# The query projection of a hybrid attention block in three product tiles per four heads, with the scaled latent split

## The chip, the cores and the metric

The kernel runs on one core of one Trainium2 chip. The time is device time in microseconds (us) of one execution, lower is better. TensorE (PE) makes the matrix products, VectorE (DVE), ScalarE (ACT) and GpSimd (POOL) the elementwise work, SyncE (SP) issues the DMAs. "PEld" in a profile is TensorE's weight load, which overlaps the products.

## The reference, cut to what matters

Two layers, each: half-step FFN, mixer, half-step FFN. The mixer of a layer reads one input `h` and makes latent attention (8 heads) beside a recurrent branch; 128 context tokens and 256 latent tokens are kept side by side as 384 columns. The part that is changed:

```
c_q, c_kv, k_rope, u_x, u_g = split(h @ w_in)
q = rms_norm(c_q, q_norm_g) @ w_uq              # 384 -> 8 heads x (64 + 32)
q_nope, q_rope = q[..., :64], q[..., 64:]
# latent tokens only:
apply_rope(x): x1, x2 = x[:16], x[16:]
               concat(x1*cos - x2*sin, x1*sin + x2*cos)
s = q_nope . k_nope + q_rope . k_rope           # then softmax, @ v
```

`rms_norm` divides by the root mean square of a token's 384 latent values and multiplies by `g`.

## The kernel before, in words

Activations are stored transposed: features on the 128 partitions, 384 tokens along the free axis (`T`). Every fp32 product is made of three rounded ones: `piece` (L307) splits a weight tile into a high part `wh` (cast on ScalarE, L315) and a low part `wl` (subtraction on VectorE, L316), activations are split in the same way, and `mm3` (L319 to L322) makes high x high, high x low and low x high. Weights come through `stage` buffers (`ws`, three of them) by DMAs that SP issues (L295); the splits go to `split_pool` (three each).

The order of the work on each engine is not written by hand: a scheduler orders the instructions by program order as a priority and its own plan of the times, and assigns buffers; each engine then works through its own list in order. Splits are marked as urgent (`PIECE_AHEAD`). A "pump" makes the modulation vectors (`gm` products from `wm`, L238) in steps that the scheduler puts between other products.

Products go to PSUM tiles: four `acc` tiles (tag `acc`), three `ms` tiles, one `gm` tile. Temporary tiles of 384 columns share the tag `t1` (three buffers): the gate branch's `gu`, the rotary product `qr`, the latent's `cq`.

The mixer in program order: the convolution and the recurrent branch (`lru`, advanced by `next(lru)` between other parts); the key/value latent; the rotary key (`krm`, `kr`); the query latent; the gate branches 0 and 1; `keys(0)`, `queries(0)`, `values()`, the gate branches 2 and 3; then the attention over head pairs, with `keys(1)` and `queries(1)` in front of the third pair; the pump's steps; the output projection (`w_o`).

The query latent, before: three chunks, each multiplied by `g` (L660) and split at once (`cqh` L661, `cql` L662), while the squares go to `token_scale`, which sums them over the partitions, takes the power on GpSimd (L352) and spreads the factor `pr` over the partitions by a product (L555). The factor is not put on the latent but on the projected queries: `rr` is the rotary table `tab` times `pr` (L665).

`queries(hf)`, before: each of four heads has a tile of 128 rows: 64 plain rows, 32 rotary ones, and the same 32 with their halves swapped, which GpSimd copies into the weights (`turn_q`, L700, L701). So a head is one product tile of three chunks, nine products, and on VectorE:

```
nc.vector.tensor_tensor(t2[64:96, P:T], ps[96:128, P:T], rr[96:128, P:T], op=ALU.mult)
nc.vector.tensor_tensor(q[0:96, :], ps[0:96, :T], rr[0:96], op=ALU.mult)
nc.vector.tensor_tensor(q[64:96, P:T], q[64:96, P:T], t2[64:96, P:T], op=ALU.add)
```

The scores (L772) then take 96 rows of `qT` and `kT`; the maxima are L773, the exponentials L778. The 32 rotary rows of `kT` are copied from `kr` by DMAs on SP (L713).

## Time and profile before

| what | value |
|---|---|
| time, median of 3 runs | 1603.82 us (1603.72 to 1605.43) |
| the profiled execution | 1606.49 us, its span 1604.7 us |
| TensorE busy | 1551.7 us, 97% of the span |
| VectorE / ScalarE / GpSimd busy | 946.9 / 659.4 / 161.3 us |
| mean granted clock of TensorE | 0.984 |

Times inside the profile are microseconds from the start of its span. Products overlap each other, so the shown duration of one is longer than the distance to the next.

### The profile page before, as it was taken

The numbers are of one execution on the slowest core, as the hardware profiler recorded it, in microseconds if no ns is written. First come the engines' busy times: TensorE is split into PE (matmuls) and PEld (weight loads), VectorE is DVE, ScalarE is ACT, GpSimd is POOL, SyncE is SP. The second block draws the span as 40 slices with busy tenths as digits, with TensorE's granted clock in tenths as the row PEclk, the third lists the DMA queues.
The fourth block names the chain that finished last, engine by engine and source line by source line (L and its number), as shares of the span: only waits on it lengthen the run. The fifth ranks groups of instructions, "written<-read, shape, count | busy, mean of one in ns | idle before, by whom it ended". The sixth has DMA issues, their size and how long they took to land.

```text
span 1604.7 us, 22948 instructions
## 1 busy us (share of the span) xinstructions
PE 1551.7 (97%) x9234; PEld 1453.5 (91%) x9234; DVE 946.9 (59%) x1568; ACT 659.4 (41%) x1068; POOL 161.3 (10%) x142
## 2 busy tenths in 40 slices
PE   6999999999999999999999999999999989999997
PEld 5999999988668999999989999998866789999996
DVE  3778754477986947864364444346788664344334
ACT  4533333268743633333243333234775444333321
POOL 0000002220004100001120000033000140000011
PEclk9999999999999999999989999999999989999998
DMA  9865553447644445553444333335654223433331
GB/s 308 268 231 188 181 200 125 117 143 244 208 156 158 159 158 181 200 191 126 141 157 156 108 132 125 125 105 171 201 186 146 74 65 125 144 120 129 120 118 40
DMA packets 214790, 249.93 MB, mean 156 GB/s; under 512 B 26394, under 2 KB 193308, under 8 KB 211612
## 3 DMA queue, kind: packets, MB, share of 16 engines
q1 hardware_dynamic: 214684, 248.47, 46.5%
q8 instruction: 72, 1.18, 0.3%
q14 instruction: 34, 0.28, 0.1%
HBM read 245.52 MB, written 1.88 MB: 154 GB/s over the span
## 4 chain that ended last, share of the span: by engine, by line
PE 91%; DVE 4%; DMA 2%; ACT 1%; POOL 1%; issue 1%; SPq 0%; DVEq 0%; ACTq 0%; POOLq 0%
PE acc L320 27%; PE acc L322 27%; PE acc L321 27%; PE gm L238 3%; PE acc L772 1%; PE ms L392 1%; DVE wl L316 1%; PE pv L805 1%; DMA wm<-in_w_mod_dram 1%; DMA ws<-in_w_ffn_up_dram 1%; PE ms L788 1%; PE ms L320 1%; PE ms L321 0%; PE ms L322 0%; POOL sum_f L378 0%
## 5 line engine op out<-in xcount | busy, mean ns | idle before, releaser
L315 ACT CAST wh<-ws 128x1024 fp32r<-128x1024 f32 (+1 forms) x332 | 336.3, 1014 | 755.3 <-PE acc L321 523.0
L316 DVE TENSOR_TENSOR wl<-ws,wh 128x1024 fp32r<-128x1024 f32 (+1 forms) x332 | 411.5, 1240 | 376.9 <-ACT wh L315 373.7
L320 PE MATMUL acc<-hh,wh 128*128 128x384 f32 x1280 | 428.8, 338 | 10.5 <-ACT hh L278 7.4
L322 PE MATMUL acc<-hh,wl 128*128 128x384 f32 x1280 | 431.9, 338 | 2.4 <-DVE wl L316 2.4
L321 PE MATMUL acc<-hl,wh 128*128 128x384 f32 x1280 | 432.5, 338 | 0.4 <-DVE hl L286 0.4
L320 PEld LDWEIGHTS acc<-hh,wh 128*128 128x128 f32 x1280 | 241.6, 189 | 17.7 <-ACT hh L278 8.6
L322 PEld LDWEIGHTS acc<-hh,wl 128*128 128x128 f32 x1280 | 243.3, 190 | 6.4 <-DVE wl L316 2.9
L321 PEld LDWEIGHTS acc<-hl,wh 128*128 128x128 f32 x1280 | 243.2, 190 | 2.6 <-issue 1.3
L320 PE MATMUL acc<-gh,wh 128*128 128x384 f32 x704 | 236.7, 336 | 0.0
L321 PE MATMUL acc<-gl,wh 128*128 128x384 f32 x704 | 236.3, 336 | 0.0
L322 PE MATMUL acc<-gh,wl 128*128 128x384 f32 x704 | 236.0, 335 | 0.0
L320 PEld LDWEIGHTS acc<-gh,wh 128*128 128x128 f32 x704 | 132.1, 188 | 0.4 <-issue 0.4
L321 PEld LDWEIGHTS acc<-gl,wh 128*128 128x128 f32 x704 | 132.3, 188 | 0.0
L322 PEld LDWEIGHTS acc<-gh,wl 128*128 128x128 f32 x704 | 132.1, 188 | 0.0
L492 DVE TENSOR_TENSOR a<-a,acc 128x384 f32<-128x384 f32 x87 | 48.2, 554 | 122.6 <-PE acc L322 117.7
L252 DVE SCALAR_TENSOR_TENSOR gsum<-wm,sil,gsum 128x512 f32<-128x512 f32 x168 | 120.0, 766 | 0.0
L320 PE MATMUL acc<-hh_in,wh 128*128 128x384 f32 x336 | 112.0, 339 | 5.2 <-ACT hh_in L278 5.0
L321 PE MATMUL acc<-hl_in,wh 128*128 128x384 f32 x336 | 113.0, 336 | 0.0
L322 PE MATMUL acc<-hh_in,wl 128*128 128x384 f32 x336 | 112.7, 336 | 0.0
L377 POOL TENSOR_TENSOR sum_f<-X 128x384 f32<-128x384 f32 x4 | 5.1, 1281 | 829.5 <-DVE X L368 829.5
L320 PEld LDWEIGHTS acc<-hh_in,wh 128*128 128x128 f32 x336 | 63.0, 189 | 7.1 <-ACT hh_in L278 6.1
L238 PE MATMUL gm<-wm,sil 128*32 128x128 f32 (+2 forms) x640 | 62.1, 446 | 4.3 <-DMA wm<-in_w_mod_dram 2.0
(268 smaller groups left out, 1750.2 us busy)
## 6 DMA issues: line engine op xcount, KB each, us to landing
ws<-in_w_ffn_up_dram SPq DMA_DIRECT2D x84, 1024.0 KB, 5.1
wm<-in_w_mod_dram SPq DMA_DIRECT2D x56, 1024.0 KB, 5.4
ws<-in_w_ffn_down_dram SPq DMA_DIRECT2D x32, 1024.0 KB, 5.2
wm<-in_w_mod_dram SPq DMA_DIRECT2D x32, 512.0 KB, 5.1
ws<-in_w_ffn_down_dram SPq DMA_DIRECT2D x16, 768.0 KB, 4.5
ws<-in_w_in_dram SPq DMA_DIRECT2D x12, 1024.0 KB, 6.1
ws<-in_w_o_dram SPq DMA_DIRECT2D x8, 1024.0 KB, 5.3
ws<-in_w_ffn_up_dram SPq DMA_DIRECT2D x8, 384.0 KB, 6.7
```

Of the source, the lines that this page charges most:

```text
L238: nc.tensor.matmul(self.ps[32 * g : 32 * g + 32, :n], lhsT, wv[:, g], start=self.fresh, stop=stop)
L252: nc.vector.scalar_tensor_tensor(self.sum[:, r], wv[:, kk], s, self.sum[:, r], op0=ALU.mult, op1=ALU.add)
L315: nc.scalar.copy(parts[0], src)
L316: nc.vector.tensor_tensor(parts[1], src, parts[0].bitcast(F32), op=ALU.subtract)
L320: nc.tensor.matmul(ps, wh, xh, start=start, stop=False)
L321: nc.tensor.matmul(ps, wh, xl, start=False, stop=False)
L322: nc.tensor.matmul(ps, wl, xh, start=False, stop=stop)
L392: nc.tensor.matmul(self.pt[:, 2 * i + j : 2 * i + j + 1], src[:, i * P : (i + 1) * P], mean_w[:, 0:1], start=False, stop=stop and i == T / ...
L492: nc.vector.tensor_tensor(a, a, px[:, :T], op=ALU.mult)
L772: nc.tensor.matmul(views[i], qT[hf][0:96, h % 4, q0 : q0 + P], kT[hf][0:96, h % 4, k0:k1], start=True, stop=True)
L788: nc.tensor.transpose(t0[:, (2 * j + i) * P : (2 * j + i + 1) * P], pr_[:, (0, 512)[i] + j * P : (0, 512)[i] + (j + 1) * P], ident)
L805: nc.tensor.matmul(o[:, P:T], v, pTs[e][:, (j - 1) * 256 : j * 256], start=(j == 1), stop=(j == 3))
```

## The change

The query latent is kept in fp32 (`cq32`, three `t1` tiles) until `pr` is there, is multiplied by it, and only then split; `rr` is gone. The weights of four heads come in one DMA of whole rows. Of four heads the 64 plain rows are taken two heads per product tile (two tiles), and the rotary rows of all four heads in a third tile, first halves in rows 0 to 63, second halves in rows 64 to 127. Plain rows are copied to `qT` (VectorE and ScalarE one each per tile); the rotary tile is turned with `cos` and `sin` tables over all 128 partitions, and eight DMAs that GpSimd issues put 16 rows each at their places in `qT`. `cos` and `sin` are built from `tab` by twelve DMAs on GpSimd's queue in place of one load on SP's. The rotary key uses the new tables, with the sign of one half put on its weight.

```diff
+    def split(parts, n):
+        n_w[0] += 1
+        th, tl = (split_pool.tile([P, 1024], F32R, tag=tag, name=f"{tag}{n_w[0]}") for tag in ("wh", "wl"))
+        with tc.high_priority(offset=PIECE_AHEAD):
+            for src, view in parts:
+                nc.scalar.copy(view(th[:, :n]), src)
+                nc.vector.tensor_tensor(view(tl[:, :n]), src, view(th[:, :n]).bitcast(F32), op=ALU.subtract)
+        return th[:, :n], tl[:, :n]
...
             def turn(ws):
                 v = ws[:, : KD * P].rearrange("p (k c) -> p k c", c=P)
                 nc.gpsimd.tensor_copy(v[:, :, 96:112], v[:, :, 80:96])
-                nc.gpsimd.tensor_copy(v[:, :, 112:128], v[:, :, 64:80])
+                nc.gpsimd.tensor_scalar(v[:, :, 112:128], v[:, :, 64:80], -1.0, None, op0=ALU.mult)
...
                 nc.vector.tensor_scalar_mul(h32, ps[:, :T], g)
+                cq32.append(h32)
+                next(lru)
+            pr = token_scale(sqs, sel_q, RMS_EPS, f"q{l}")
+            for j, h32 in enumerate(cq32):
+                nc.vector.tensor_tensor(h32, h32, pr[:, :T], op=ALU.mult)
                 nc.scalar.copy(cqh[:, j, :], h32)
                 nc.vector.tensor_tensor(cql[:, j, :], h32, cqh[:, j, :].bitcast(F32), op=ALU.subtract)
-                next(lru)
-            pr = token_scale(sqs, sel_q, RMS_EPS, f"q{l}")
-            nc.vector.tensor_tensor(rr, tab, pr[:, :T], op=ALU.mult)
...
             def queries(hf):
...
+                q = qT[hf]
+                n = 4 * (DN + DR)
+                w = load_w([(lambda t: t[:, : 3 * n].rearrange("p (k c) -> p k c", c=n), w_uq[:, :, n * hf : n * hf + n])])
+                w = w[:, : 3 * n].rearrange("p (k h e) -> p k h e", k=3, h=4)
+                wh, wl = split([(w[:, :, :, :DN], lambda t: t.rearrange("p (k h e) -> p k h e", k=3, h=4))], 3 * 4 * DN)
...
+                for j in range(2):
                     ps = acc_tile()
                     for k in range(3):
-                        mm3(ps[:, :T], wh[:, k, o : o + P], wl[:, k, o : o + P], cqh[:, k, :], cql[:, k, :], k == 0, k == 2)
...
+                        mm3(ps[:, :T], wh[:, k, j * P : (j + 1) * P], wl[:, k, j * P : (j + 1) * P], cqh[:, k, :], cql[:, k, :], k == 0, k == 2)
+                    nc.vector.tensor_copy(q[0:64, 2 * j, :], ps[0:64, :T])
+                    nc.scalar.copy(q[0:64, 2 * j + 1, :], ps[64:128, :T])
+                wh, wl = split([(w[:, :, :, DN + 16 * x : DN + 16 * x + 16],
+                                 lambda t, x=x: t.rearrange("p (k x h e) -> p k x h e", k=3, x=2, h=4)[:, :, x]) for x in range(2)], 3 * P)
...
+                t1, t2 = (tmp.tile([P, T], F32, tag="t1", bufs=3, name=f"qr{i}{l}{hf}") for i in range(2))
+                nc.vector.tensor_tensor(t1, ps[:, :T], cos, op=ALU.mult)
+                nc.vector.tensor_tensor(t2[0:64, P:T], ps[64:128, P:T], sin[64:128, P:T], op=ALU.mult)
+                nc.vector.tensor_tensor(t2[64:128, P:T], ps[0:64, P:T], sin[0:64, P:T], op=ALU.mult)
+                nc.vector.tensor_tensor(t1[:, P:T], t1[:, P:T], t2[:, P:T], op=ALU.add)
+                for h in range(4):
+                    for x in range(2):
+                        nc.gpsimd.dma_start(q[64 + 16 * x : 80 + 16 * x, h, :], t1[64 * x + 16 * h : 64 * x + 16 * h + 16])
...
-    tab = const.tile([P, T], F32, name="tab")
-    nc.sync.dma_start(tab, A["tab"])
+    cos, sin = (const.tile([P, T], F32, name=n) for n in ("cos", "sin"))
+    for i in range(4):
+        nc.gpsimd.dma_start(cos[32 * i : 32 * i + 32], A["tab"][64:96])
+    for i in range(8):
+        r0 = 112 if i < 4 else 96
+        nc.gpsimd.dma_start(sin[16 * i : 16 * i + 16], A["tab"][r0 : r0 + 16])
```

## Rows read from the trace of the kernel before

**Rows 1.** The page: engines' busy time, and the chain that ended last.
```profile
PE 1551.7 (97%) x9234; PEld 1453.5 (91%) x9234; DVE 946.9 (59%) x1568; ACT 659.4 (41%) x1068; POOL 161.3 (10%) x142
...
PE 91%; DVE 4%; DMA 2%; ACT 1%; POOL 1%; issue 1%; SPq 0%; DVEq 0%; ACTq 0%; POOLq 0%
```

**Rows 2.** TensorE's timeline, layer 0, second query group: start, duration, instruction.
```profile
452.11 0.44 PE L320 MATMUL acc<-cqh,wh 128*128 128x384 f32 x1
...
458.51 1.25 PE L772 MATMUL acc<-kT,qT 96*128 96x128 f32 x6
```

**Rows 3.** Windows: busy time per engine (instructions), granted clock, DMA share, GB/s.
```profile
400.00:420.00 20.00, 19.18 (x104) 14.89 (x103) 18.63 (x32) 17.77 (x26) 1.26 (x2) 1.00 0.60 210
460.00:475.00 15.00, 14.72 (x83) 7.61 (x76) 12.83 (x38) 7.94 (x28) 0.00 (x0) 1.00 0.70 253
1246.00:1260.00 14.00, 11.01 (x50) 6.70 (x49) 11.54 (x35) 6.09 (x24) 0.00 (x0) 0.88 0.17 60
```

**Rows 4.** TensorE's waits in layer 1's mixer: total, times, longest.
```profile
PE acc L772 <- ACT p L778: 1.9, 1, 1.9
...
PE acc L772 <- DVE qT L739: 1.0, 1, 1.0
```

**Rows 5.** TensorE's timeline, layer 0, first query group; in brackets idle time and releaser.
```profile
410.09 0.45 PE L320 MATMUL acc<-cqh,wh 128*128 128x384 f32 x1 [0.59 <-DVE gu L679]
...
418.19 0.47 PE L320 MATMUL acc<-wh,ckh 128*128 128x512 f32 x1 [0.23 <-DVE qT L739]
...
429.36 1.90 PE L772 MATMUL acc<-kT,qT 96*128 96x128 f32 x8
```

**Rows 6.** VectorE's groups by form: count, busy time, mean ns, idle time before.
```profile
L316 DVE TENSOR_TENSOR wl<-ws,wh 128x768 fp32r<-128x768 f32 x48 | 45.9, 957 | 110.2 <-ACT wh L315 110.2
...
L739 DVE TENSOR_TENSOR qT<-acc,rr 96x384 f32<-96x384 f32 x16 | 8.9, 554 | 0.2
...
L738 DVE TENSOR_TENSOR qr<-acc,rr 32x256 f32<-32x256 f32 x16 | 6.8, 428 | 1.6 <-PE acc L322 1.0
L740 DVE TENSOR_TENSOR qT<-qT,qr 32x256 f32<-32x256 f32 x16 | 6.7, 420 | 0.4
...
L710 DVE COPY kT<-acc 64x512 f32<-64x512 f32 x8 | 5.4, 679 | 2.3 <-PE acc L322 2.3
...
L662 DVE TENSOR_TENSOR cql<-cq,cqh 128x384 fp32r<-128x384 f32 x6 | 3.3, 548 | 0.1
```

**Rows 7.** VectorE's timeline, layer 0, around the query latent's factor.
```profile
396.52 0.55 DVE L679 SCALAR_TENSOR_TENSOR gu<-gu,acc 128x384 f32<-128x384 f32 x1
398.34 0.56 DVE L665 TENSOR_TENSOR rr<-tab,ms 128x384 f32<-128x384 f32 x1 [1.27 <-PE ms L555]
...
401.01 0.96 DVE L316 TENSOR_TENSOR wl<-ws,wh 128x768 fp32r<-128x768 f32 x1 [0.32 <-ACT wh L315]
...
403.23 0.68 DVE L710 COPY kT<-acc 64x512 f32<-64x512 f32 x1 [0.80 <-PE acc L322]
```

**Rows 8.** One line of the kernel, SP's copies of `kr`: duration of issue, time to landing.
```profile
L713 SPq DMA_DIRECT2D kT<-kr x16: 571/588/624, 366.6 to 1230.9; - x16
...
DMA to landing us min/median/max: 2.0/3.0/5.8
```

**Rows 9.** Timelines of ScalarE (layer 0, layer 1) and VectorE (layer 1), second group's softmax.
```profile
463.94 0.37 ACT L778 ACTIVATE p<-acc,mx 128x128 f32<-128x128 f32 x1 [4.36 <-DVE mx L774]
...
1250.29 0.37 ACT L778 ACTIVATE p<-acc,mx 128x128 f32<-128x128 f32 x1 [4.28 <-DVE mx L774]
...
1247.73 2.32 DVE L773 TENSOR_REDUCE mx<-acc 128x1 f32<-128x384 f32 x5
```

**Rows 10.** TensorE's timeline, layer 0, among the second group's scores.
```profile
462.99 1.92 PE L238 MATMUL gm<-wm,sil 128*32 128x512 f32 x14
```

**Rows 11.** The opening: a window as in rows 3, and the chain in time order.
```profile
0.00:40.00 40.00, 27.21 (x321) 23.61 (x321) 13.89 (x48) 16.73 (x31) 0.68 (x6) 1.00 0.93 308
...
17.00 8.88 DMA ws<-in_w_ffn_up_dram
```

More of the change, by code (lines that the diff above doesn't have):

```diff
@@ L565, in mixer @@
             kr = mp.tile([P, 512], F32, name=f"kr{l}")
-            rr = mp.tile([P, T], F32, name=f"rr{l}")
             ckh = mp.tile([P, 2, 512], F32R, name=f"ckh{l}")
@@ L646, in mixer @@
             next(lru)
-            sqs = []
+            sqs, cq32 = [], []
             for j in range(3):
@@ L695, in mixer @@
             w_kv = load_w(parts).rearrange("p (k s c) -> p k s c", k=2, s=2)
-            w_uq = A["w_uq"][l].rearrange("(k p) (h e) -> p k h e", p=P, h=H)
-            def turn_q(ws):
-                v = ws[:, :1536].rearrange("p (x e) -> p x e", e=P)
-                nc.gpsimd.tensor_copy(v[:, :, 96:112], v[:, :, 80:96])
-                nc.gpsimd.tensor_copy(v[:, :, 112:128], v[:, :, 64:80])
+            w_uq = A["w_uq"][l].rearrange("(k p) c -> p k c", p=P)
             def keys(hf):
@@ L725, in queries @@
                 qT[hf] = qkv.tile([P, 4, T], F32, tag="qT", name=f"qT{l}{hf}")
-                parts = [(lambda t, k=k: t[:, k * 512 : (k + 1) * 512].rearrange("p (h e) -> p h e", e=P)[:, :, :96],
-                          w_uq[:, k, 4 * hf : 4 * hf + 4]) for k in range(3)]
-                w = load_w(parts, turn_q)[:, :1536].rearrange("p (k c) -> p k c", k=3)
-                for j in range(4):
-                    if j % 2 == 0:
-                        wh, wl = piece(w[:, :, j * P : (j + 2) * P])
-                    o = (j % 2) * P
+                q = qT[hf]
@@ L733, in queries @@
+                n = 4 * (DN + DR)
+                w = load_w([(lambda t: t[:, : 3 * n].rearrange("p (k c) -> p k c", c=n), w_uq[:, :, n * hf : n * hf + n])])
+                w = w[:, : 3 * n].rearrange("p (k h e) -> p k h e", k=3, h=4)
+                wh, wl = split([(w[:, :, :, :DN], lambda t: t.rearrange("p (k h e) -> p k h e", k=3, h=4))], 3 * 4 * DN)
+                wh, wl = (x.rearrange("p (k c) -> p k c", k=3) for x in (wh, wl))
+                for j in range(2):
                     ps = acc_tile()
@@ new lines, in queries @@
+                    nc.vector.tensor_copy(q[0:64, 2 * j, :], ps[0:64, :T])
+                    nc.scalar.copy(q[0:64, 2 * j + 1, :], ps[64:128, :T])
+                wh, wl = split([(w[:, :, :, DN + 16 * x : DN + 16 * x + 16],
+                                 lambda t, x=x: t.rearrange("p (k x h e) -> p k x h e", k=3, x=2, h=4)[:, :, x]) for x in range(2)], 3 * P)
+                wh, wl = (x.rearrange("p (k c) -> p k c", k=3) for x in (wh, wl))
+                ps = acc_tile()
+                for k in range(3):
+                    mm3(ps[:, :T], wh[:, k], wl[:, k], cqh[:, k, :], cql[:, k, :], k == 0, k == 2)
```

9 lines of the change are left out of this document (2 added, 7 removed).

## The prediction

> **What bounds the kernel now.** I read the page first. TensorE is busy 97% of the span and the chain that ended last runs on it for 91% [rows 1]: what leaves the chain must be TensorE work, and what returns must be a wait of TensorE. The two mixers hold the whole change, so I then read TensorE in order of time through the first one. A product of 384 columns shows about 0.34 us, but such instructions overlap. The pace is what counts: 36 of them run from 452.11 to the first scores at 458.51 [rows 2], so 6.40 / 36 = 0.178 us each. The reader should see that a removed product is worth 0.178 us, not 0.34.
>
> Third, the waits. In the 15 us of that second group's scores TensorE idles 0.28 us in layer 0 (15.00 - 14.72); in layer 1 it idles 2.99 of 14 us and the mean granted clock is 0.88 [rows 3]. There the waits are for the softmax's exponentials on ScalarE (1.9 us) and for `qT` (1.0 us) [rows 4]: a chain of latencies, not TensorE's work, sets that stretch. Fourth, the stretch of the first query group: VectorE is busy 18.63 of 20 us and TensorE 19.18 [rows 3]. Two engines are near full there, and the only waits of TensorE from 404 us to the first scores are for VectorE to give back a PSUM tile: 0.59 us for the gate branch's `gu`, 0.23 us for `qT` [rows 5].
>
> **The change, part by part.** *TensorE.* Per four heads the before kernel makes four product tiles (nine products each), the changed one three. Over two groups and two layers that is 4 x 9 = 36 products less: 36 x 0.178 = **-6.4 us**. This is certain as work, and as time only while TensorE doesn't wait instead.
>
> *VectorE behind the products.* Before, each tile costs 0.428 + 0.554 + 0.420 us [rows 6], 5.6 us per four heads. After: two plain copies (at most the 0.68 us of the `kT` copy [rows 6], which has more columns; I take 0.55), one multiplication over 384 columns (0.55), two over 256 (0.43 each), one sum (0.42): 2.9 us. The other two plain copies go to ScalarE, which is less full than VectorE there [rows 3]. The weight split shrinks from 2 x 768 columns (0.957 each [rows 6]) to 768 and 2 x 192; a 192-column split isn't in the trace, it lies between 0 and the 0.957 of 768 columns; by its length I take 0.3. So VectorE gains some 3 us per four heads. That is worth only the 0.23 us wait for `qT` in the first group [rows 5]: **-0.2 us**. The weights come in one transfer instead of three and lose two GpSimd copies; both finish long before use, so nothing is gained.
>
> *The latent, scaled and then split.* The factor reaches VectorE at 398.34 [rows 7]. Before, the three splits of `cq` were long done and only one multiplication followed (`rr`, 0.56). After, three multiplications (0.554 each, as `qT`'s of 384 columns [rows 6]), three ScalarE casts and three subtractions (0.548 [rows 6]) come behind it: 3 x 0.554 + 3 x 0.548 - 0.56 = 2.75 us more VectorE in exactly the full stretch. It also keeps all three `t1` buffers until then, so the first gate branch's two steps (2 x 0.55 us, the last at 396.52 [rows 7]) slide behind it too: 3.85 us. VectorE has idle spots of 0.32 and 0.80 us there [rows 7], which leaves 2.7 us. Queued behind are the `kT` copies, the scans and the second `gu`; for that one a query tile waits until 410.09 (0.59 us [rows 5]), and for want of a PSUM tile TensorE can only do pump products meanwhile. Bounds per layer: 0 (the wait is filled) and 3.85 us; I take half of 2.7, since the order is planned anew and ScalarE's `kT` copies free two other tiles: 2 x 1.35 = **+2.7 us**.
>
> *Rotary rows by DMA.* New: behind the rotary product 0.55 + 2 x 0.43 + 0.42 = 1.83 us of VectorE, then eight GpSimd DMAs of 16 partitions, two per head. The trace has no DMA issued by GpSimd; the nearest row is `kT` from `kr` on SP: 0.59 us per issue, 3.0 us to landing, 5.8 at most [rows 8]. First group: the products end about 415, the first scores start at 429.36 [rows 5]. 1.8 + 8 x 0.59 + 3.0 = 9.5 us fit into 14: hidden by the value and gate products; without that cover it would be the second group's case. There nothing lies between. Layer 1: the products end at 1244.94 - 1.6 = 1243.3, VectorE at 1245.2, the first head's two transfers at 1245.2 + 0.6 + 3.0 = 1248.8, then scores and maxima, some 2.5 us (by 1247.73, where five maxima begin, and the exponentials at 1250.29 [rows 9]), so exponentials at 1251.3 against 1250.29. That is 1.0 later instead of 1.6 earlier: +2.6. Layer 0: 458.51 - 1.6 + 1.8 + 3.6 = 462.3, exponentials at 464.8 against 463.94 [rows 9]; but the pump's products stand among the scores there (14 of 512 columns at 462.99 [rows 10]) and TensorE hardly idles, so they fill the wait: 0. Together **+2.6 us**, between 0 and the late case below. Behind the DMAs on GpSimd's queue come only the residual's sums, after the attention; each copy of `t1` is held until its DMAs have landed, and nothing but two gate branches asks for one of the other two.
>
> The Trainium skill (DMA: Bandwidth & Descriptors, Anatomy of one DMA — SWDGE (gpsimd) path) gives a GpSimd DMA a fixed 2.0 us plus a bytes term, by which 24 KB land in an estimated 2.1 us; the row of an SP transfer says 3.0, no row here shows GpSimd's, and by the page the sum would be 0.9 us less.
>
> *Opening.* `tab` (one SP load behind the opening's weights) becomes twelve GpSimd loads, 256 rows of 1536 bytes, 393 KB together. GpSimd has nothing else then, so they may start with the first weights, where the DMA engines move 308 GB/s at a share of 0.93 and the chain waits 8.88 us for an up-projection load [rows 11]. 393 KB / 308 GB/s = 1.28 us; bounds 0 and 1.28, I take half: **+0.6 us**. The key's sign flip costs GpSimd one instruction in place of another of the same size: 0.
>
> **Sum.** -6.4 - 0.2 + 2.7 + 2.6 + 0.6 = -0.7 us. The profiled execution took 1606.49 us (span 1604.7), 2.67 above the median; -0.7 on it is 1605.8, and on the median 1603.82 it is **1603.1 us**.
>
> **Rivals.**
> *The saving comes through.* The planner finds products for both first-group waits, and layer 1's transfers cost only 1.0 us: -6.4 - 0.2 + 1.0 + 0.6 = -5.0, **1598.8 us**. For it: TensorE is the bound almost everywhere [rows 1], and VectorE gets lighter. Against: the waits have hardly any work but the pump that needs no PSUM tile.
> *Late rotary rows (slower).* If GpSimd issues at 1.2 us and lands at the slowest row's 5.8 [rows 8], the second group's first head is ready 1.2 + 5.8 behind VectorE: 7.0 instead of 3.6: exponentials at 1254.7 and 468.2, 4.4 and 4.3 later than now, so +6.0 and, with the pump used up, +5.9: -6.4 - 0.2 + 2.7 + 11.9 + 0.6 = +8.6, **1612.4 us**. It decides from about 4.3 us of issue and landing in both layers (the sum passes +3.2 there). For it: both layers have the scores directly behind, and layer 1's stretch already shows a granted clock of 0.88, so a longer wait may cost clock too. Against: `kT`'s median is half of it.
> The Trainium skill (SBUF — State Buffer, SBUF: two separate sides) speaks for this case: VectorE operations in a two-port mode lock GpSimd out, so that it can't write descriptors, and a transfer of 620 ns took 3100. No row here shows a GpSimd DMA beside VectorE.
> *VectorE's queue in full.* Both first groups wait the whole 3.85, and the opening the whole 1.28: -6.4 - 0.2 + 7.7 + 2.6 + 1.3 = +5.0, **1608.8 us**. For it: VectorE at 18.63 of 20 us [rows 3].
> *No effect of the change at all* is excluded: 36 products are gone from the list.
>
> **Chances.** Forecast (part given back) 0.42, saving comes through 0.31, VectorE's queue 0.12, late rows 0.15. A measurement of this kernel can tell 0.2%, 3.2 us. Faster: 0.31 and 0.03 of the forecast's spread, 0.34. Slower: 0.15 and 0.08 of the queue's case, 0.23. Within: the rest, 0.43. The range has to reach into both signs: 1597.0 (a little under the second case, since its +1.0 may be 0) to 1609.5 leaves out about 0.08 below and 0.12 above. The forecast's own range is 1600 to 1606.
>
> **What would show it.** Right: 108 instead of 144 products from `cqh` and `cql`; a wait of 1 to 3 us before the second query tile in both layers, its releaser VectorE; the first scores of layer 1's second group some 5 us behind the last query product, waiting for a DMA; the first group's scores not waiting. Wrong: GpSimd issues or landings far from 0.6 and 3.0 us; another releaser than a `gu` step near 410; scores of layer 0's second group idling TensorE; the twelve table loads not in the opening; or a new order that moves waits into stretches the change doesn't touch.

## The result, and the profile after

The changed kernel takes 1632.03 us (median of 4, 1625.30 to 1633.14) beside 1604.39 us for the kernel before on the same chip: ratio 1.0153, interval 1.0138 to 1.0168. It is slower: by some 25 us by the ratio and between the two profiled executions (spans 1629.7 and 1604.7 us), by 27.6 between the medians. Forecast were 1603.1 us, a range from 1597.0 to 1609.5, and a chance of 0.23 for slower. The range did not hold the time.

The page of the changed kernel, engines' busy time and the chain that ended last:

```profile
span 1629.7 us, 22947 instructions
...
PE 1554.8 (95%) x9198; PEld 1453.9 (89%) x9198; DVE 935.0 (57%) x1552; ACT 661.6 (41%) x1080; POOL 179.7 (11%) x178
...
PE 91%; DVE 3%; ACT 2%; DMA 2%; POOL 1%; issue 1%; SPq 0%; DVEq 0%; POOLq 0%; ACTq 0%
```

Beside [rows 1]: TensorE runs 36 products fewer and is busy 3 us longer, in a span 25 us longer. Less work has become more busy time, so the products themselves got slower (an estimate: 36 products fewer at 0.175 us should have taken 6.3 us off, so some 9.4 us are new); and some 22 us are new idle time (span less busy: 74.9 against 53.0). To see where, I took the first product of each stage from the timelines of both kernels:

| stretch, us | before | changed | before, with rotary rows by transfer (12) | changed, rotary tile first (9) | as 9, products for transfers and loads (14) |
|---|---|---|---|---|---|
| opening, to the first down-projection product | 221.7 | 225.9 | 223.2 | 225.4 | 222.1 |
| to the first query product | 182.7 | 182.3 | 183.5 | 183.8 | 184.6 |
| layer 0, first query to last output product | 111.3 | 126.6 | 121.8 | 111.3 | 108.0 |
| to layer 1's first query product | 673.7 | 673.2 | 670.3 | 669.7 | 670.4 |
| layer 1, first query to last output product | 111.6 | 118.8 | 121.9 | 114.8 | 110.3 |
| the rest of the span | 303.7 | 302.9 | 304.3 | 303.0 | 303.8 |

(The last three columns are experiments below.) Of the 25 us, 15.3 are lost in layer 0's mixer, 7.2 in layer 1's, 4.2 in the opening; the rest gives 1.7 back. TensorE's waits in the changed kernel (total, times, longest):

```profile
PE acc L789 <- DMA qT<-qr: 15.5, 2, 9.0
...
PE acc L330 <- ACT kT L717: 5.3, 2, 2.6
```

These two lines are new: the scores waiting for the rotary rows' transfers, once per layer, and a product waiting for ScalarE's copy of `kT`, once per layer. The two mixers as windows (columns as in [rows 3]), of the kernel before:

```profile
404.40:515.70 111.30, 109.05 (x607) 84.52 (x606) 92.95 (x186) 54.72 (x116) 19.97 (x14) 0.98 0.52 178
1189.40:1301.00 111.60, 105.91 (x590) 83.29 (x588) 83.09 (x171) 54.97 (x116) 18.39 (x14) 0.98 0.36 121
```

and of the changed kernel:

```profile
408.20:534.80 126.60, 113.33 (x609) 85.76 (x608) 90.02 (x186) 59.05 (x124) 25.54 (x28) 0.93 0.53 176
1208.00:1326.80 118.80, 107.07 (x578) 83.21 (x576) 79.46 (x166) 59.16 (x124) 25.54 (x28) 0.94 0.35 117
```

Window less busy PE (its first figure) is idle time; one less the granted clock, times the window, is about what the half level took (an estimate: at 1.2 GHz a product of the first group goes at 0.32 us instead of 0.175, shown below). Layer 0: idle 13.27 against 2.25, +11.0; clock 0.07 x 126.6 - 0.02 x 111.3, +6.6. Layer 1: idle 11.73 against 5.69, +6.0; clock 7.1 - 2.2, +4.9. But these two terms overlap. Part of the half level falls on the long waits themselves, where TensorE has no work to slow down; two windows inside the waits:

```profile
472.40:478.20 5.80, 0.00 (x1) 0.04 (x1) 2.39 (x5) 0.00 (x0) 2.97 (x7) 0.50 1.06 354
1267.70:1272.00 4.30, 0.00 (x0) 0.00 (x0) 1.34 (x2) 0.00 (x0) 2.31 (x5) 0.50 0.73 239
```

Half of their lengths, 2.9 and 2.2 us, is counted twice and comes off the clock, which leaves +3.7 and +2.7 (an estimate). Eighteen query products less are worth -3.2 in each layer. That makes +11.5 of the 15.3 measured in layer 0 and +5.5 of 7.2 in layer 1. Most of the rest is work that the new order moved into these stretches: 14 more pump products in layer 0 (86 instead of 72) and six more products of the recurrent branch in each layer (an estimate: 22 pump products take 2.77 us in layer 0 of the kernel before, a product of the branch 0.175, so 2.8 and 1.0 us). So the saving is there, and waits and the clock take it back several times over; about a quarter of that loss in layer 0 and a third in layer 1 is clock, the rest is waiting.

Cut at the first scores of each mixer, the part ahead of them (the first group, from the first query product on) grew by 5.7 us in layer 0 and 4.9 in layer 1, the part behind them by 9.6 and 2.3. Layer 0's first group as a window, before and changed:

```profile
404.40:429.30 24.90, 24.08 (x134) 20.02 (x133) 24.45 (x47) 18.08 (x30) 1.26 (x2) 1.00 0.63 214
408.20:438.90 30.70, 28.07 (x147) 21.62 (x146) 24.15 (x47) 21.48 (x35) 3.96 (x8) 0.94 0.81 266
```

**Layer 0's second group.** TensorE's timeline of the changed kernel, which answers to [rows 2]:

```profile
467.04 0.33 PE L332 MATMUL acc<-cqh,wl 128*128 128x384 f32 x1
467.31 1.92 PE L238 MATMUL gm<-wm,sil 128*32 128x512 f32 x16
478.20 2.04 PE L789 MATMUL acc<-kT,qT 96*128 96x128 f32 x4 [8.97 <-DMA qT<-qr]
```

The last query product, sixteen pump products, and then nothing for 8.97 us. VectorE's timeline of that gap:

```profile
467.90 0.55 DVE L751 TENSOR_TENSOR qr<-acc,cos 128x384 f32<-128x384 f32 x1
468.46 0.43 DVE L752 TENSOR_TENSOR qr<-acc,sin 64x256 f32<-64x256 f32 x1
468.90 0.42 DVE L753 TENSOR_TENSOR qr<-acc,sin 64x256 f32<-64x256 f32 x1
469.35 1.23 DVE L316 TENSOR_TENSOR wl<-ws,wh 128x1024 fp32r<-128x1024 f32 x1
470.49 0.42 DVE L754 TENSOR_TENSOR qr<-qr,qr 128x256 f32<-128x256 f32 x1
```

The four operations cost what was forecast (1.82 against 1.83 us), but a weight split of 1024 columns stands between the third and the fourth. Then GpSimd's timeline, where one line is the eight transfers' issue together:

```profile
471.56 3.81 POOL L757 DMA_DIRECT2D qT<-qr  x8 [41.27 <-DVE gmt L230]
```

the chain in order of time, in layer 0 and in layer 1:

```profile
472.03 5.92 DMA qT<-qr
...
1270.16 1.68 DMA qT<-qr
```

and all transfers of `qT` together:

```profile
L757 POOL DMA_DIRECT2D qT<-qr x32: 484/484/625, 426.3 to 1273.0; - x32
...
DMA to landing us min/median/max: 1.7/5.2/6.5
```

One issue is 0.48 us, less than the 0.59 taken from [rows 8]. Landing is the matter: 1.68 us in layer 1, 5.92 in layer 0. The windows around the two:

```profile
470.00:480.00 10.00, 1.80 (x4) 1.26 (x5) 5.79 (x14) 0.00 (x0) 3.81 (x8) 0.62 0.96 317
...
1265.00:1285.00 20.00, 12.72 (x49) 7.64 (x50) 12.19 (x31) 7.22 (x22) 3.81 (x8) 0.74 0.20 63
```

In layer 0 the sixteen DMA engines are 0.96 full (317 GB/s, mostly weights that SP loads), in layer 1 0.20. The same 24 KB take 3.5 times as long beside full engines, and not only this once: all eight transfers of layer 0's second group landed in 4.9 to 5.9 us, all eight of layer 1's in 1.7 to 1.8. The Trainium skill (DMA: Bandwidth & Descriptors, Anatomy of one DMA — SWDGE (gpsimd) path) gave an estimated 2.1 us; layer 1's 1.68 is near it, layer 0's 5.92 is not. The other page of the Trainium skill cited with the forecast (SBUF — State Buffer, SBUF: two separate sides) would have GpSimd locked out beside VectorE operations in a two-port mode. The issues here took 0.484 to 0.625 us each beside VectorE's operations; no run shows the mode of these, so the rule is not tested.

**The clock.** In both windows the granted clock is below full speed (0.62 and 0.74): it is at the half level (0.50) during TensorE's standstill, as shown above, and still when the scores run (0.50 from 478.2 to 482.6). The same shows at the first group's small wait, in TensorE's timeline of layer 0, which answers to [rows 5]:

```profile
417.02 0.44 PE L330 MATMUL acc<-cqh,wh 128*128 128x384 f32 x1 [2.63 <-ACT kT L717]
...
418.23 0.52 PE L332 MATMUL acc<-cqh,wl 128*128 128x384 f32 x1
418.55 0.52 PE L330 MATMUL acc<-cqh,wh 128*128 128x384 f32 x1
```

After 2.63 us without work the products start, from the fifth on and until 421.1, 0.32 us apart; in the second group, behind uninterrupted work, they start 0.175 apart.

**The opening.** First FFN product of the changed kernel, at 18.96 us before:

```profile
21.84 1.65 PE L330 MATMUL acc<-hh_in,wh 128*128 128x384 f32 x4 [3.08 <-ACT hh_in L278]
```

DMA issues of the tables (count, KB each, median us to landing):

```profile
cos<-in_tab_dram POOLq DMA_DIRECT2D x4, 48.0 KB, 5.2
sin<-in_tab_dram POOLq DMA_DIRECT2D x8, 24.0 KB, 6.3
```

The twelve loads go out with the first weights, and the first product is 2.9 us later, not the 0.6 forecast.

### The profile page after: what moved, and what is told of

Its sections match the earlier page's. It is cut to its first block, busy times and chain, and to the rows that moved or that the text cites. A ratio compares the mean times of both kernels' runs of the same rounds, so it can differ in the third digit from the quotient of the medians.

```text
span 1629.7 us, 22947 instructions
## 1 busy us (share of the span) xinstructions
PE 1554.8 (95%) x9198; PEld 1453.9 (89%) x9198; DVE 935.0 (57%) x1552; ACT 661.6 (41%) x1080; POOL 179.7 (11%) x178
## 4 chain that ended last, share of the span: by engine, by line
PE 91%; DVE 3%; ACT 2%; DMA 2%; POOL 1%; issue 1%; SPq 0%; DVEq 0%; POOLq 0%; ACTq 0%
PE acc L330 27%; PE acc L332 27%; PE acc L331 27%; PE gm L238 3%; PE acc L789 1%; PE ms L402 1%; DVE wl L316 1%; DMA wm<-in_w_mod_dram 1%; PE pv L822 1%; PE ms L330 1%; PE ms L331 1%; ACT wh L315 1%; PE ms L332 0%; DMA qT<-qr 0%; PE ms L805 0%
## 5 line engine op out<-in xcount | busy, mean ns | idle before, releaser
L315 ACT CAST wh<-ws 128x1024 fp32r<-128x1024 f32 (+1 forms) x324 | 329.6, 1019 | 741.9 <-PE acc L331 499.6
L316 DVE TENSOR_TENSOR wl<-ws,wh 128x1024 fp32r<-128x1024 f32 (+1 forms) x324 | 406.0, 1254 | 382.2 <-ACT wh L315 376.8
```

Of the source, the lines that this page charges most:

```text
L315: nc.scalar.copy(parts[0], src)
L316: nc.vector.tensor_tensor(parts[1], src, parts[0].bitcast(F32), op=ALU.subtract)
```

## The experiments

Ratios are to the kernel before on the same chip. "Changed" is the changed kernel, 1.0153.

**1. Table loads on SP's queue**
```
-        nc.gpsimd.dma_start(cos[32 * i : 32 * i + 32], A["tab"][64:96])
+        nc.sync.dma_start(cos[32 * i : 32 * i + 32], A["tab"][64:96])
```
(and so for `sin`)

> The changed kernel with its twelve table loads issued by SP, behind the opening's weights, instead of by GpSimd at the start. Theory (the early loads compete with the first weights): the opening gets back about 4 us, first product tile of the up-projection near 19 us instead of 21.8, time about 1628. Rival (the opening's delay comes from the new order of the work, not from these loads): the opening stays, time about 1632.

Measured 1628.44 us, ratio 1.0144 [1.0127, 1.0160], which the changed kernel's interval overlaps. The first FFN product is back at 18.9 us, but the first down-projection product starts at 229.5 instead of 225.9: the twelve issues now stand in front of SP's weight loads. The opening's loss moved; it did not go. So the time is the expected one, but not for the expected reason.

**2. No transfers: four engine copies instead**
```
-                for h in range(4):
-                    for x in range(2):
-                        nc.gpsimd.dma_start(q[64 + 16 * x : 80 + 16 * x, h, :], t1[64 * x + 16 * h : 64 * x + 16 * h + 16])
+                for h in range(4):
+                    (nc.scalar.copy if h % 2 else nc.vector.tensor_copy)(q[64:96, h, :], t1[32 * h : 32 * h + 32])
```
The copies move 32 partitions as they lie, so other rotary rows than the reference's enter the scores.

> The changed kernel with the eight DMAs per four heads replaced by four engine copies of 32 partitions (two on VectorE, two on ScalarE); they take other rows than the reference's, so the rotary part of the scores is another one. Theory (the rotary rows arrive late): the waits of 9.0 and 6.6 us before the second group's scores shrink to about 2 each, time 1632 - 12 = 1620 or less. Rival (the rotary arithmetic behind the product and the order planned around it are late anyway): waits of 5 us stay, time about 1627.

Measured 1614.85 us, ratio 1.0054 [1.0038, 1.0070]: 16 us less than the changed kernel by the ratios. TensorE's waits before the second groups' scores, layer 0 and layer 1:

```profile
PE acc L788 <- DVE qT L756: 2.7, 1, 2.7
...
PE acc L788 <- ACT qT L756: 4.2, 1, 4.2
```

The waits fall from 9.0 and 6.6 us to 2.7 and 4.2, 8.7 us together, and the time by nearly twice as much. In the stretch between the mixers, where no instruction differs, this kernel is 5.4 us shorter too; that part is taken up at the end.

**3. Kernel before, with the latent scaled and then split**
```
-                nc.scalar.copy(cqh[:, j, :], h32)
-                nc.vector.tensor_tensor(cql[:, j, :], h32, cqh[:, j, :].bitcast(F32), op=ALU.subtract)
+                cq32.append(h32)
...
+            for j, h32 in enumerate(cq32):
+                nc.vector.tensor_tensor(h32, h32, pr[:, :T], op=ALU.mult)
+                nc.scalar.copy(cqh[:, j, :], h32)
+                nc.vector.tensor_tensor(cql[:, j, :], h32, cqh[:, j, :].bitcast(F32), op=ALU.subtract)
-            nc.vector.tensor_tensor(rr, tab, pr[:, :T], op=ALU.mult)
+            rr = tab
```

> The kernel before with one part of the change: the query latent is kept until the factor is there, scaled and then split; the four product tiles per four heads stay and are multiplied by the plain table. Theory (the first group's loss of 5.8 and 4.9 us comes from the scaled latent, which holds three buffers and fills VectorE): time 1604 + 8 to 11 = 1613. Rival (that loss comes from the new product tiles, whose release is shared by ScalarE): time 1604 to 1607.

Measured 1607.39 us, ratio 1.0009 [0.9991, 1.0027]. The forecast's +2.7 us lies in that interval, and so does no change. The wait for `gu` is 1.9 and 2.0 us, as forecast (1 to 3, releaser VectorE). But the first groups, from the first query product to the first scores, take 29.2 and 29.1 us here, against 25.0 and 25.6 in the kernel before: part of their growth comes with this edit alone, and in part it is work that the new order moved there (six more products of the recurrent branch in each).

**4. Kernel before, with its table in eight GpSimd loads**
```
-    nc.sync.dma_start(tab, A["tab"])
+    for i in range(8):
+        nc.gpsimd.dma_start(tab[16 * i : 16 * i + 16], A["tab"][16 * i : 16 * i + 16])
```

> The kernel before with its one table load on SP replaced by eight loads of 16 rows on GpSimd, at the start: 192 KB early, half of what the changed kernel loads. Theory (small early loads delay the first weights): 2 to 4 us more, time 1606 to 1608, the first product of the opening near 20 to 22 us instead of 19. Rival (they are hidden): 1604.

Measured 1607.37 us, ratio 1.0012 [0.9997, 1.0028]: half the bytes of the change's twelve loads, first FFN product at 20.0 instead of 19.0 us, first down-projection product 2.4 us later, and at most some 4.5 us of it at the end. Not told apart from no effect.

**5. Transfers issued by ScalarE**
```
-                        nc.gpsimd.dma_start(q[64 + 16 * x : 80 + 16 * x, h, :], t1[64 * x + 16 * h : 64 * x + 16 * h + 16])
+                        nc.scalar.dma_start(q[64 + 16 * x : 80 + 16 * x, h, :], t1[64 * x + 16 * h : 64 * x + 16 * h + 16])
```

> The rotary rows go out by ScalarE's queue instead of GpSimd's; nothing else changes. If the long landing (5.9 and 1.7 us on the chain, median 5.2) belongs to GpSimd's way of sending, the waits before the second groups' scores fall from 9.0 and 6.6 us to some 5 each and the time to 1621 to 1627 us. If the rows are late because of the weight loads that fill the DMA engines beside them, the landing stays at 4 to 6 us and the time at 1629 to 1633. If ScalarE's own eight issues come behind its other work, the waits grow and the time passes 1634.

Measured 1631.90 us, ratio 1.0168 [1.0151, 1.0185]. The median landing is 4.8 us instead of 5.2, the one on the chain in layer 0 5.44 instead of 5.92, and the waits are 8.2 and 6.5 us. It is not GpSimd's way of sending; the rows are late by either queue.

**6. Rotary operations and transfers at the chain's priority**
```
+                with tc.high_priority(offset=CHAIN_AHEAD):
+                    nc.vector.tensor_tensor(t1, ps[:, :T], cos, op=ALU.mult)
...
```

> The four VectorE operations on the rotary tile and the eight transfers get the chain's priority, so that the split of an output weight (1.23 us, one in layer 0's second group, one or two in layer 1's) no longer stands between them. If that split is what the prediction left out, each second group's wait falls by 1.2 to 2.5 us and the time by 3 to 6, to 1626 to 1629 us. If the waits are set by issue and landing alone, they stay at 9.0 and 6.6 and the time within 2 us of 1632.

Measured 1627.07 us, ratio 1.0140 [1.0120, 1.0160], not told apart from the changed kernel. The edit missed its aim: the split of 1.23 us still stands between the third operation and the sum, in both layers. The waits are 7.4 and 6.6 us; of the 1.6 us that went in layer 0, 0.7 is the transfer's landing (5.24 us), the rest that eighteen instead of sixteen pump products stand in front of the wait. The time lies where it was expected if the split moved, but the split did not move; what it costs by itself stays unmeasured.

**7. Rows placed by a product, in the transfers' place**
```
-                        nc.gpsimd.dma_start(q[64 + 16 * x : 80 + 16 * x, h, :], t1[64 * x + 16 * h : 64 * x + 16 * h + 16])
+                pp = misc_tile()
+                nc.tensor.matmul(pp[:, :T], perm, t1, start=True, stop=True)
+                for h in range(4):
+                    (nc.scalar.copy if h % 2 else nc.vector.tensor_copy)(q[64:96, h, :], pp[32 * h : 32 * h + 32, :T])
```
`perm` is the identity with its columns reordered.

> The rotary rows are put in place by a product with a column-permuted identity (once per four heads, four passes of 384 columns) and four copies, two on VectorE and two on ScalarE; no transfers. If the transfers' wait and the fall of the clock behind it are the main loss, the waits come down to some 3 to 4 us (2.7 and 4.2 with plain copies) and the time to 1614 to 1619 us. If the loss is in the longer chain of copies and the latent, it stays above 1625.

Measured 1629.13 us, ratio 1.0152 [1.0137, 1.0168]: no gain, where both readings of "the transfers are the loss" wanted 12 us or more. TensorE's timeline of layer 0's second group in this kernel:

```profile
467.34 1.92 PE L238 MATMUL gm<-wm,sil 128*32 128x512 f32 x16
471.09 0.88 PE L758 MATMUL ms<-qr,perm 128*128 128x384 f32 x2 [1.83 <-DVE qr L756]
472.67 6.31 PE L792 MATMUL acc<-kT,qT 96*128 96x128 f32 x12 [0.69 <-issue]
...
480.76 3.49 PE L792 MATMUL acc<-kT,qT 96*128 96x128 f32 x6 [1.78 <-ACT p L798]
```

and that mixer as a window:

```profile
407.60:531.10 123.50, 115.85 (x613) 86.62 (x612) 92.83 (x192) 61.10 (x128) 17.61 (x12) 0.93 0.52 178
```

No wait in this mixer is over 3 us now (in layer 1's, one is 3.7). Yet the idle time is still 7.65 us, 5.4 more than before, in pieces; the clock is 0.93, as in the changed kernel; and the scores between the pieces take longer (twelve in 6.31 us): from 472.3 to 486.0 the clock is at 0.50 and TensorE busy for 11.55 of the 13.7 us. Taking the long wait away is not enough while the chain still hangs behind the last product. This contradicted the theory as I had it, "the transfers are the loss", and led to run 9.

**8. The latent split unscaled, the factor multiplied into the query**
```
+                nc.scalar.copy(cqh[:, j, :], h32)
+                nc.vector.tensor_tensor(cql[:, j, :], h32, cqh[:, j, :].bitcast(F32), op=ALU.subtract)
...
-                    nc.vector.tensor_copy(q[0:64, 2 * j, :], ps[0:64, :T])
-                    nc.scalar.copy(q[0:64, 2 * j + 1, :], ps[64:128, :T])
+                    nc.vector.tensor_tensor(q[0:64, 2 * j, :], ps[0:64, :T], rr[0:64], op=ALU.mult)
+                    nc.vector.tensor_tensor(q[0:64, 2 * j + 1, :], ps[64:128, :T], rr[64:128], op=ALU.mult)
...
+                nc.vector.tensor_tensor(t1, t1, rr, op=ALU.mult)
```

> The latent is split unscaled, as before, and the token factor is multiplied into the query tiles (the nope copies all on VectorE, one more VectorE multiplication of the rotary tile); the three tiles and the transfers stay. If the scaled latent costs what the scaled latent alone cost (1.0009 of before, 1 to 2 us), the time falls by no more than 3 us, to 1629 to 1633. If the 4.9 and 5.8 us that the first groups lost come from the scaled latent, the time falls to 1619 to 1624. If the extra VectorE work lies ahead of the rotary rows, the second groups' waits grow by 0.5 to 1 us each.

Measured 1622.05 us, ratio 1.0113 [1.0088, 1.0138]: some 6 us less than the changed kernel by the ratios. The first groups (first query product to first scores) shrink to 23.5 and 23.6 us from 30.7 and 30.5; the kernel before has 25.0 and 25.6. The wait for ScalarE's `kT` copy is gone, a wait for `gu` of 1.4 us is there. Behind the first groups part of it is lost again (the waits for the transfers are 8.4 and 7.5 us, and layer 0's mixer still takes 122.3 us).

**9. The rotary tile first of the three** (its block of lines, unchanged, stands ahead of the other two tiles')
```
-                wh, wl = split([(w[:, :, :, :DN], lambda t: t.rearrange("p (k h e) -> p k h e", k=3, h=4))], 3 * 4 * DN)
...
-                    nc.scalar.copy(q[0:64, 2 * j + 1, :], ps[64:128, :T])
                 wh, wl = split([(w[:, :, :, DN + 16 * x : DN + 16 * x + 16],
...
                         nc.gpsimd.dma_start(q[64 + 16 * x : 80 + 16 * x, h, :], t1[64 * x + 16 * h : 64 * x + 16 * h + 16])
+                wh, wl = split([(w[:, :, :, :DN], lambda t: t.rearrange("p (k h e) -> p k h e", k=3, h=4))], 3 * 4 * DN)
...
+                    nc.scalar.copy(q[0:64, 2 * j + 1, :], ps[64:128, :T])
```

> The rotary tile is made first of the three, the two others behind it; all else as in the changed kernel, the transfers too. Eighteen products then stand between the rotary tile's end and the scores (3.2 us at 0.18 us, 5.8 at the 0.32 us of the lower clock), and one split. If lateness of the rotary rows is the main loss, the waits of 9.0 and 6.6 us fall to 3 to 6 and 1 to 3, and the time to 1620 to 1626 us. If the transfers land late whenever they start, or the clock falls all the same, it stays above 1628.

Measured 1611.87 us, ratio 1.0048 [1.0030, 1.0065]: 17 us less by the ratios, by a change of order alone, and below every time that was expected. The waits for the transfers in this kernel, layer 0 and layer 1:

```profile
PE acc L789 <- DMA qT<-qr: 1.4, 1, 1.4
...
PE acc L789 <- DMA qT<-qr: 4.4, 1, 4.4
```

and the mixers as windows:

```profile
409.20:520.50 111.30, 105.60 (x582) 80.77 (x581) 87.48 (x175) 56.42 (x121) 26.47 (x28) 0.98 0.54 181
1190.20:1305.00 114.80, 106.34 (x564) 82.35 (x563) 77.17 (x160) 56.18 (x121) 25.54 (x28) 0.94 0.36 121
```

The kernel has the same products, copies and transfers, with eighteen products behind the rotary chain instead of none: layer 0's mixer is back at the 111.3 us of the kernel before, with its clock of 0.98. A part of that is work that the new order put elsewhere (64 pump products in this window instead of 86), so the kernel's whole time is the safer measure. In layer 1 the gain is in the first group (25.9 us instead of 30.5); behind it the transfers still cost 4.4 us of waiting, the clock is 0.94, and nothing is won.

**10. Rotary tile first, rows by a product, latent unscaled** (the edits of 7, 8 and 9 together)

> Three repairs at once: the latent split unscaled, the rotary tile first, and its rows placed by a product and four copies in place of transfers (one product of four passes per four heads more, some 0.7 us each). If waits in front of in-order products and the clock behind them are the whole loss, no wait over 2 us is left around the query groups, the 36 products less come through as 3 to 4 us, and what is left is the opening: 1603 to 1610 us. If the repairs only add (10 us of the unscaled latent, 3 of the product), it is 1617 to 1621; if the clock falls for another reason than these waits, above 1615.

Measured 1613.46 us, ratio 1.0051 [1.0031, 1.0071]. Both mixers are below the kernel before (110.9 and 109.3 us), but the stretch between them is 676.7 us and the opening 225.8: what the mixers gain is lost in stretches that the edits don't touch. It fell between the outcomes that were laid out.

**11. As 10, the tables from one load and two products**
```
-    for i in range(4):
-        nc.gpsimd.dma_start(cos[32 * i : 32 * i + 32], A["tab"][64:96])
...
+    nc.sync.dma_start(tab, A["tab"])
+    for dst, cols in ((cos, [(0, 8, 64)]), (sin, [(0, 4, 112), (4, 4, 96)])):
...
+        nc.tensor.matmul(ps[:, :T], sel_t, tab, start=True, stop=True)
+        nc.vector.tensor_copy(dst, ps[:, :T])
```

> As the run before it, and the two tables are no longer loaded by twelve transfers: one load of the rotary table as in the kernel before, and two products with 0/1 columns of the identity that repeat its rows. If the twelve loads cost the opening its 4 us for good, this is 2 to 4 us below the run before it, and the first FFN product starts at 19 to 20 us. If the opening's loss is given back later (as it was with eight loads alone, ratio 1.0012), it is within 1.5 us.

Measured 1604.46 us, ratio 1.0004 [0.9988, 1.0020]. The first FFN product is at 19.0 us, the first down-projection product at 223.4. By the medians this is 9 us below run 10, more than either outcome allowed. The two profiled executions are only 3.8 us apart (spans 1609.2 and 1605.4): 2.4 in the opening, 1.1 in layer 0's mixer and 5.6 between the mixers, less 3.0 in layer 1's mixer, 1.7 ahead of the first query product and 0.6 at the end, where run 10 is the faster. So what the tables by themselves are worth is not shown by this pair.

**12. Kernel before, with its rotary rows placed by transfers**
```
...
-                    nc.vector.tensor_tensor(q[0:96, :], ps[0:96, :T], rr[0:96], op=ALU.mult)
-                    nc.vector.tensor_tensor(q[64:96, P:T], q[64:96, P:T], t2[64:96, P:T], op=ALU.add)
+                    nc.vector.tensor_tensor(t1[64:96], ps[64:96, :T], rr[64:96], op=ALU.mult)
+                    nc.vector.tensor_tensor(q[0:64, :], ps[0:64, :T], rr[0:64], op=ALU.mult)
+                    nc.vector.tensor_tensor(t1[64:96, P:T], t1[64:96, P:T], t2[64:96, P:T], op=ALU.add)
+                    for x in range(2):
+                        nc.gpsimd.dma_start(q[64 + 16 * x : 80 + 16 * x], t1[64 + 16 * x : 80 + 16 * x])
```
It also adds one VectorE operation to each tile.

> The kernel before, with one thing of the change: each head's 32 rotary rows are computed into a buffer and two GpSimd transfers put them into the query. Four tiles, the unscaled latent and the table stay. If the transfer in front of in-order products is the main loss, waits of 4 to 8 us for a transfer appear before the second groups' scores, with a lower clock behind, and the time is 1614 to 1622 us. If the changed kernel's loss came from the latent and the order around it, this stays at 1604 to 1609.

Measured 1626.13 us, ratio 1.0129 [1.0106, 1.0152]: most of the changed kernel's loss, with four tiles, the old latent and the old table. But not as expected: the waits put down to a transfer are 2.3 and 0.4 us. The mixers as windows:

```profile
406.70:528.50 121.80, 114.43 (x613) 85.84 (x612) 97.71 (x194) 55.11 (x116) 26.65 (x30) 0.96 0.53 175
1198.80:1320.70 121.90, 115.78 (x590) 88.77 (x588) 87.75 (x179) 55.24 (x116) 26.25 (x30) 0.90 0.34 114
1262.20:1275.90 13.70, 12.44 (x31) 7.47 (x30) 9.85 (x28) 5.60 (x20) 0.99 (x3) 0.50 0.13 40
```

In layer 1 TensorE idles only 6.12 us, 0.4 more than before, with the same 590 products. The granted clock is 0.90 instead of 0.98: 12.2 - 2.2 = 10.0 us by the estimate above, of the 10.3 us by which that mixer is longer. Here the half level falls on work, not on a wait: the third line is the longest stretch at 0.50, with TensorE busy for 12.44 of 13.7 us, and the mixer's busy time is 9.9 us longer than before (115.78 against 105.91). The waits there are many and short (four of 0.3 to 1.0 us among the second group's scores), and the clock falls all the same. A profile of waits alone would have put this mixer at no loss. In layer 0's mixer both parts grow (idle time by 5.1 us).

**13. As 9, the tables from one load and two products**

> The changed kernel with the rotary tile first and the tables repeated by two products instead of twelve loads; the scaled latent and the transfers stay. If the twelve loads cost the opening for good, this is 3 to 6 us below the run with the rotary tile first alone (1611.9), at 1606 to 1609 us; if their loss is given back, 1610 to 1613.

Measured 1610.96 us, ratio 1.0036 [1.0018, 1.0054], in an interval that overlaps run 9's. First FFN product at 18.9 us, first down-projection product 224.6 against 225.4. What the twelve loads cost at the end is not told apart from nothing here. (The profiled execution is one of the fastest of its kernel, 1604.92 us, so its stages are not those of the median.)

**14. As 11, the latent scaled** (three tiles, rotary tile first, products for transfers and loads)

> Three tiles with the rotary tile first, its rows by a product, the tables by products; the scaled latent stays. Beside the same kernel with the unscaled latent (1604.5, ratio 1.0004): if the scaled latent costs its 5 us in each first group also when nothing waits for rotary rows, this is at 1609 to 1615 us. If that loss was only the wait that the last tile's rows made behind it, it is within 2 us of 1604.5, and the ratio to before is below 1.001. If scaling ahead of the split is a gain once the waits are gone (nothing left to multiply behind the products), 1600 to 1603.

Measured 1603.63 us, ratio 0.9989 [0.9978, 1.0001]. Its mixers:

```profile
406.70:514.70 108.00, 105.38 (x593) 79.85 (x593) 88.09 (x181) 58.09 (x124) 17.94 (x12) 1.00 0.57 193
1185.10:1295.40 110.30, 104.52 (x567) 81.71 (x567) 78.81 (x164) 57.73 (x124) 17.84 (x12) 0.97 0.35 122
```

Layer 0's mixer idles 2.62 us at a clock of 1.00, 3.3 us shorter than before; layer 1's is 1.3 us shorter. Not all of the 3.3 are the products: run 4, whose mixers are those of the kernel before, takes 109.8 us for layer 0's at a clock of 1.00, 1.8 us more than here. That is near what 18 products less and two placing products more should give in a mixer (an estimate: 18 x 0.175 - 2 x 0.64 = 1.9 us); layer 1's window holds eight pump products fewer and a lower clock (0.97), so it does not settle it. In the whole time the gain is at the bound of what can be told from no change. Run 11, the same with the latent unscaled, has an overlapping interval: once nothing hangs behind the last tile, scaling costs nothing that can be told.

## Why the prediction was wrong

**What held.** The 36 products are gone (36 instead of 48 for each of the three kinds), and in the second group they still start 0.175 us apart, so -6.4 us of work was right. VectorE's rotary operations cost 1.82 us, an issue 0.48 instead of 0.59. The first group's scores waited for no transfer. Layer 1's second group looks as described: its scores wait for a DMA, 6.58 us, starting 6.9 us behind the last query product where some 5 were forecast. That nearness is partly luck: the transfer landed 1.3 us sooner than forecast (1.68), and a weight split (1.2) and the hand-overs between the engines (1.8), which the forecast did not count, more than made up for it.

**The step that failed: layer 0's second group at 0.** The prediction let the pump's products fill that wait, because [rows 10] show them among the scores. TensorE takes its instructions in a fixed order. The changed kernel's order has sixteen pump products in front of the waiting scores, none behind them can pass, and the engine stood for 8.97 us. The largest wait of the change was costed at nothing, and the part of layer 0's mixer behind the first scores, which should have been shorter by nine products, grew by 9.6 us.

**The rotary chain was too short.** Landing was taken as 3.0 us, from [rows 8]. It is 1.7 us beside quiet DMA engines and 5.9 beside full ones (share 0.96). The window [rows 3] already gave that stretch of the kernel before a share of 0.70. The split of 1024 columns between the third and fourth VectorE operation (1.23 us) was not counted. Nor were the hand-overs: 0.86 us from the last product's start to VectorE's first operation, 0.65 from VectorE's last to GpSimd's first issue, 0.25 from landing to scores. With all of these, layer 0 runs from the last query product to the scores in 11.2 us, where the steps of the forecast (1.8 + 0.6 + 3.0) give 5.4.

**Late rotary rows was the nearest rival.** It had 0.15 and 1612.4 us. Its place was right: it counted both second groups as late, with the pump used up in layer 0, at +5.9 and +6.0 us before the saved products. The parts behind the first scores grew by 9.6 and 2.3 us with 1.6 us of products saved in each, so some 15 us were lost there against its 11.9. It had no term for the clock, which it mentioned for layer 1 without a number, and it took the first groups and the opening over from the forecast, at +2.7 and +0.6; most of what it missed lies there.

**The term that was missing: the clock.** In the two mixers the windows give 11.0 + 6.0 us of idle time and, where TensorE had work, some 3.7 + 2.7 us for the lower level; over the whole span it is some 9.4. Run 12 separates the two: layer 1's mixer loses 10 us there with almost no more idle time. In run 7 layer 0's long wait is cut into pieces, and the clock is as low as in the changed kernel. What cures layer 0 is work behind the chain: run 9 changes the order only, and 17 us of the whole come back.

**First groups.** Forecast: +2.7 us for both, a wait of 1 to 3 us, releaser a `gu` step of VectorE. In the kernel before with this one edit (run 3) the wait is so. In the changed kernel the wait is 2.6 us in each layer, but released by ScalarE's `kT` copy, and the clock falls behind it. The first groups grow by 5.7 and 4.9 us, although nine products fewer are in each. An estimate at the prices above: idle time (2.63 us instead of 0.82 in layer 0) and clock (0.94 instead of 1.00) cost some 3.5 us in each, to be compared with +1.35, and some 3 us in each are products that the new order moved there (16 and 14 more of the pump, six more of the recurrent branch). Run 8 undoes the scaled latent and the first groups are shorter than before; but runs 11 and 14 differ in the latent alone and not in time. Its price depends on what stands behind it, and it isn't a constant to add.

**The opening.** Forecast +0.6, at most 1.28 us by bytes. The first FFN product is 2.9 us late and the first down-projection product 4.2. Bytes were the wrong measure: twelve small loads ahead of the first weights delay these by more than their own 393 KB. How much is left at the end isn't settled: runs 4, 9 and 13 allow anything from 0 to some 4 us, and 10 against 11, 9 us apart by the medians, differ by 2.4 us in the opening of the profiled executions and mostly elsewhere.

**What stays open.** Between the mixers no instruction is changed (up to 22 of the pump's products move into it or out of it), and yet that stretch takes 673 to 677 us in some kernels (before, changed, 7, 10) and 667 to 671 in the others. It goes with the clock. Windows in the changed kernel, and in run 2 around the same work:

```profile
1100.00:1130.00 30.00, 27.49 (x139) 20.25 (x139) 12.77 (x24) 8.84 (x17) 4.83 (x5) 0.83 0.53 172
```

```profile
1087.00:1117.00 30.00, 28.02 (x170) 23.95 (x169) 15.79 (x28) 10.88 (x21) 6.51 (x6) 1.00 0.63 208
```

0.17 x 30 = 5.1 us, about the difference of 5.4 us between the two. What makes the clock fall there in some kernels wasn't found, so a few us in each comparison above, of run 7 with run 2 in particular, are not the edit's own. One profile per kernel can't tell whether it is the kernel or the execution. The times and clocks of the other executions say that executions of one kernel differ in the same way: run 13's twelve lie between 1604.1 us at a mean granted clock of 0.987 and 1617.8 at 0.979, and the changed kernel's four between 1625.3 at 0.979 and 1633.1 at 0.973. In run 13, 0.008 of the clock is 12.9 of the 13.6 us, by the estimate above. So a comparison of stages from one profile each is good to a few us, and the ratios are what the comparisons between kernels rest on.

## What to carry to other kernels

Put the tile with the longest chain behind it first in its group, so that the other tiles' products run while its rows are on the way: here the order alone gave back 17 of 25 us, while another queue, a priority and a product in place of the transfers, each with the tile last, gave nothing that could be told. (Plain copies in place of the transfers gave 16 us, but they put other rows there.) On an engine with a fixed order, count work as cover only if it stands behind the waiting instruction's producer and in front of the wait. Price a new wait of TensorE with the clock behind it, and read a transfer's landing for the DMA share of the moment in which it is sent, not from the median of another.

## What the runs showed of the hardware that was not expected

- The clock can cost more than the waits before it: run 12's layer 1 mixer has 0.4 us more idle time and a mean granted clock of 0.90 instead of 0.98, 10 us longer. What preceded and accompanied its longest stretch at the half level were four pauses of 0.3 to 1.0 us among short score products. In the changed kernel part of the half level falls on the long wait itself and costs nothing there.
- The same 24 KB transfer from SBUF to SBUF landed in 1.7 us with the DMA engines 0.20 busy and in 5.9 us with them 0.96 busy; sent from ScalarE's queue it took 5.4 us at that place.
- Twelve loads of 48 and 24 KB from GpSimd at the start land in 5.2 and 6.3 us (median) and put the first FFN product off by 2.9 us; moved to SP's queue they leave it at 18.9 us and put the first down-projection product off by 7.8 us instead of 4.2.
